# First layer of a two-layer decoder trunk: latent rows turned by VectorE's blocks and HBM, latent products seven units later, the attentions' first scores moved

## The chip, the core and the metric

The kernel runs on one core of one Trainium2 chip. Its engines are TensorE (PE, products; PEld is its weight load), VectorE (DVE), ScalarE (ACT), GpSimd (POOL), and SyncE (SP), which only issues DMAs; SPq is its DMA queue. Each engine runs its own list of instructions in order and waits for the others by semaphores. The metric is the device time of the whole program in microseconds (us), median of the runs shown; lower is better.

## The reference

```python
def hybrid_mixer(h, w_in, ...):
    p = h @ w_in
    (cq, ckv, k_rope, mq, mk, mv, rq, rk, rv, rg, g_mla, g_moba, g_ret) = jnp.split(p, IN_SPLIT_IDX, axis=-1)
    o_mla = mla_branch(cq, ckv, k_rope, mla_q_norm, mla_kv_norm, mla_w_q_up, mla_w_kv_up, cos_mla, sin_mla)
    o_moba = moba_branch(mq, mk, mv, cos_moba, sin_moba)
    o_ret = retention_branch(rq, rk, rv, rg, ret_gn_w, ret_gn_b, cos_ret, sin_ret)
    merged = (jax.nn.sigmoid(g_mla) * (o_mla @ w_branch_mla)
              + jax.nn.sigmoid(g_moba) * (o_moba @ w_branch_moba)
              + jax.nn.sigmoid(g_ret) * (o_ret @ w_branch_ret))
    return merged @ w_out
...
def mla_branch(cq, ckv, k_rope, q_norm_g, kv_norm_g, w_q_up, w_kv_up, cos, sin):
    cq = rms_norm(cq, q_norm_g)
    ckv = rms_norm(ckv, kv_norm_g)
    q = (cq @ w_q_up)            # 8 heads of 64 + 32 (rope on the 32)
    kv = (ckv @ w_kv_up)         # 8 heads of 64 (keys) + 64 (values)
    ...                          # rope(k_rope) is shared by the heads
    o = causal_attention(q, k, v, (MLA_NOPE + MLA_ROPE) ** -0.5)
...
for l in range(DEPTH):           # 2 layers; 256 rows of 1024
    h = rms_norm(x, attn_norm[l])
    x = x + hybrid_mixer(h, w_in[l], ...)
    h = rms_norm(x, mlp_norm[l])
    x = x + jnp.square(jax.nn.relu(h @ w_mlp_up[l])) @ w_mlp_down[l]
return rms_norm(x, final_norm)
```

The latent rows are cq (256 columns), ckv (128) and k_rope (32): normalised (the first two) or roped (the third), they are multiplied by the latent weights w_q_up and w_kv_up. With 256 rows, the moba branch is a causal attention of 8 heads of 64 with rope on 16 of the 64. All is float32.

## The kernel before

**Tiling.** The 256 rows are two halves of 128, the width of 1024 is 8 chunks of 128. A weight block is 128 x 1024 numbers, 512 KB. `weight_plan` (line 72 on) lists all blocks in the order of use; SP fetches them into `raw` (7 buffers), ScalarE rounds each to its upper half `whi` (line 287), VectorE subtracts to get the lower half `wlo` (line 289), 6 buffers each. PE makes three products of each pair (upper by upper, upper by lower, lower by upper: `three`, lines 308 to 310). A **unit** is the work on one block: 12 products of 512 columns. A projection of 512 columns is four units (j = 0 to 3) that sum into two accumulator banks, and its `done` step copies them out. There are four banks `acc` and four banks `misc`, each taken in turn, so a bank's next user waits for the copy that empties it.

**The order.** `prog` is the list of units; `at(slot(key, j), step)` hangs a step behind a unit; `run` goes through it once. At the build a scheduler turns this into one list per engine, with its own estimates of durations, except for what is pinned to program order. In layer 0 the units are: `start` 0 to 7 (the latent columns and mq), mk 0 to 3, mv 0 to 3 with the latent units `qrope`, `qnope`, `kvup` among them, gmla0 and gmla1 (the gate of the MLA branch, whose tanh `th` stands in line 695), gmoba0 and gmoba1, rqk, rv, rg, gret0 and gret1, then the branches, `wout` and the MLP.

**Latent rows.** `c_norms` leaves them as rows (`c` and, for the roped k_rope, `krx`). PE needs them turned, as `cTh` and `cTl` (upper and lower half). In layer 0 `c_turn`, at mk 2, turns them by eight PE transposes into two misc banks `pct` (line 956) and splits them from there with the norm's gain (lines 324, 325). In layer 1 VectorE turns them in blocks of 32 x 32 into `cblocks` (line 842), one DMA writes those to HBM (`rowsbounce`, line 844), four read them back so that the whole is turned (`c_fetch`, `read_turned`, line 512, into `cT`), and a plain split follows (line 329); the gain is there multiplied into the latent weights (lines 279 to 283).

**The latent units.** `qrope` makes the rotary part of the queries (`pqr`, copied to `qr`, line 993; `swapped` exchanges quarters by four DMAs into `qkoth`; `qr_rope`, line 1011, writes the roped result into `Q`), `qnope` the rest of `Q`, `kvup` the keys `KK` and values `vml`. `pqr` and `kvup` use misc banks, `qnope` uses acc banks.

**Moba rows.** `moba_rope` ropes mq or mk as rows on VectorE (`rope_rows`, lines 494 to 497), turns them (line 338) and writes them to HBM (line 504); `fetch_turned` reads them back (line 512) as `mqT` and `mkT`; `order_queries` copies mqT into `qkT` on ScalarE (line 520) for the scores.

**Attentions.** `attention` hangs the first four heads' scores at `first`, the other four at `first + gap`, and the turning, writing and reading back of the probabilities at `first + turn` and `first + moved`. The retention branch's turned rows are `rqkT`.

Of the kernel before, what the change touches and what calls it, by code (L numbers as in the profile page):

```python
# [14 lines left out]
P = 128  # L15
D = 1024
S = 256
# [10 lines left out]

TURNED = 2, 3, 0, 1
SEVEN = [(0, 1, 2, 3, 4, 6)] * L  # L30
LATENT = {"qrope": 0, "qnope": 0, "kvup": 2}
EPS = 1e-6
GN_EPS = 1e-5
# [39 lines left out]
def weight_plan():  # L73

    plan = []

    def block(key, name, kt, cols, per):
        for j in range(0, kt, per):
            plan.append(((*key, j // per), name, (j, per), cols))

    def span(c, n):
        return range(c, c + n)

    for l in range(L):
        if l == 0:

            plan.append(((l, "mq", 0), "w_in", (0, 1), C_MQ))
            plan.append(((l, "b0", 0), "w_in", (0, 1), C_MLA))
            for k in range(1, KD):
                plan.append(((l, "b0mq", k), "w_in", (k, 1), [*C_MLA, *C_MQ]))  # L90
        else:
            for j in TURNED:
                plan.append(((l, "b0", j), "w_in", (2 * j, 2), C_MLA))
            block((l, "mq"), "w_in", KD, C_MQ, 2)
        block((l, "mk"), "w_in", KD, C_MK, 2)
        block((l, "mv"), "w_in", KD, C_MV, 2)
        start = len(plan) - 4 + l
        for i, (key, name, kt, cols) in enumerate(
            (("qrope", "mla_w_q_up", 2, C_QROPE), ("qnope", "mla_w_q_up", 2, C_QNOPE), ("kvup", "mla_w_kv_up", 1, C_KV))
        ):  # L100
            block((l, key), name, kt, cols, kt)
            plan.insert(start + 2 * i, plan.pop())
        for i in range(2):
            block((l, "gmla%d" % i), "w_in", KD, span(C_GMLA + 512 * i, 512), 2)
        for i in range(2):
            block((l, "gmoba%d" % i), "w_in", KD, span(C_GMOBA + 512 * i, 512), 2)
        def branch_block(name, i):
            block((l, "b%s%d" % (name, i)), "w_branch_" + name, 4, span(512 * i, 512), 2)

        block((l, "rqk"), "w_in", KD, C_RQK, 2)  # L110
        block((l, "rv"), "w_in", KD, C_RV, 2)
        block((l, "rg"), "w_in", KD, span(C_RG, 512), 2)
        for i in range(2):
            block((l, "gret%d" % i), "w_in", KD, span(C_GRET + 512 * i, 512), 2)
        for name, i in LATE:
            branch_block(name, i)
        for n in range(KD):
            block((l, "wout", n), "w_out", KD, span(P * n, P), KD)
        for kind, i in mlp_order(l):
            if kind == "down" and l < L - 1 and i >= NF - ENDS[l]:  # L120
                half, m = divmod(i - NF + ENDS[l], 2)
                plan.append(((l, "end", half, m), "w_mlp_down", (NF - ENDS[l] + 2 * m, 2), span(512 * half, 512)))
            elif kind == "up":
                g, j = divmod(i, 4)
                plan.append(((l, "up", g, j), "w_mlp_up", (2 * j, 2), span(512 * g, 512)))
            else:
                plan.append(((l, "down", i, 0), "w_mlp_down", (i, 1), range(D)))
    at, offset = {}, 0
    for key, name, (j, n), cols in plan:
        at[key] = (offset, n, len(cols))  # L130
        offset += P * n * len(cols)
    return plan, at, offset
# [15 lines left out]
G_CQ = 0  # L148
# [6 lines left out]
def trunk(ctx: ExitStack, tc: tile.TileContext, gx, wts, consts, gfin, gn, xtok, out):  # L155
# [112 lines left out]
    def fetch(key):  # L268
        if key[1] == "down" and key[2] // 4 in SEVEN[key[0]] and key[2] % 4 > 1:
            return fetch_sums(key)  # L270
        offset, n, c = where[key]
        sz = n * c
        raw = started.pop(key, None)
        if raw is None:
            raw = wp.tile([P, 1024], F32, name="raw", bufs=RAW)
            transfer(key, raw)
        hi = wp.tile([P, 1024], F32R, name="whi", bufs=6)
        lo = wp.tile([P, 1024], F32R, name="wlo", bufs=6)
        if key[0] and key[1] in LATENT:
            parts = [slice(c * j, c * j + c) for j in range(n)]  # L280
            for j, cs in enumerate(parts):
                fetched.append(split(raw[:, cs], hi[:, cs], lo[:, cs], gain(G_CQ + 3 * key[0] + LATENT[key[1]] + j))[0])
            return tuple(part[:, :sz].rearrange("p (k c) -> p k c", k=n) for part in (hi, lo))
        edge = {"b0mq": 416, "mq": 256}.get(key[1], sz) if key[0] == 0 else sz
        parts = (slice(0, edge), slice(edge, sz)) if edge < sz else (slice(0, sz),)
        for cs in parts:
            fetched.append(nc.scalar.activation(hi[:, cs], raw[:, cs], AF.Copy))  # L287
        for cs in parts:
            nc.vector.tensor_sub(lo[:, cs], raw[:, cs], hi[:, cs].bitcast(F32))  # L289
        return (  # L290
            hi[:, :sz].rearrange("p (k c) -> p k c", k=n),
            lo[:, :sz].rearrange("p (k c) -> p k c", k=n),
        )
# [18 lines left out]
    def gain(c):  # L312
        return G[:, c : c + 1]
# [14 lines left out]
    def split_plain(src, hi, lo):  # L328
        return nc.scalar.activation(hi, src, AF.Copy), nc.vector.tensor_sub(lo, src, hi.bitcast(F32))  # L329
# [467 lines left out]
    def layer(l, xn, before):  # L797
# [21 lines left out]
        def c_norms():  # L819
# [4 lines left out]
            for t, (ct, m) in enumerate(c0):  # L824
# [9 lines left out]
                    nc.vector.tensor_copy(dst[:, :, 16 * i : 16 * i + 16], kr[:, 0, :, :])  # L834
                for i, cs in enumerate((slice(0, MLA_QR), slice(MLA_QR, MLA_QR + MLA_KVR))):
                    nc.vector.tensor_scalar(ct[:, cs], ct[:, cs], m[:, 4 + i : 5 + i], s, op0=ALU.mult, op1=ALU.mult)
            if not l:
                return
            blocks = blocks_tile("c")
            for t, (ct, _) in enumerate(c0):  # L840
                for js, row in ((slice(0, 3), ct[:, :384]), (slice(3, 4), krx[t])):
# [99 lines left out]
        def c_turn():  # L941
# [1 line left out]
            mla["Q"] = sb.tile([P, MLA_H, S], F32, name="Q", bufs=1)  # L943
            KK = mla["K"] = sb.tile([P, MLA_H, S], F32, name="KK", bufs=1)
            mla["v"] = [w2k("vml") for _ in range(NT)]
            if l:
                parts = (c[key][:, 0:3, :].rearrange("p j (t a e) -> p (j t) a e", t=NT, a=4) for key in ("h", "l"))
                split_plain(c["T"][:, 0:3].rearrange("p j t a e -> p (j t) a e"), *parts)
                kr = w2k("kr")[:, :S]
                nc.scalar.copy(kr.rearrange("p (t a e) -> p t a e", t=NT, a=4), c["T"][:, 3])  # L950
            else:
                pts = [misc_tile("pct") for _ in range(2)]
                for k in range(4):
                    for t in range(NT):
                        o = pts[k // 2][:, (k % 2) * S + P * t : (k % 2) * S + P * t + P]
                        nc.tensor.transpose(o, c0[t][0][:, P * k : P * k + P] if k < 3 else krx[t], ident)
                for k in range(3):
                    pt = pts[k // 2][:, (k % 2) * S : (k % 2) * S + S]
                    split(pt, c["h"][:, k, :], c["l"][:, k, :], gain(G_CQ + k))
                kr = pts[1][:, S:]  # L960
            for rows, odd in ((slice(0, 64), 1), (slice(64, P), 0)):
                nc.scalar.copy(KK[rows, odd::2, :], kr[rows, None, :].to_broadcast([64, 4, S]))

        if l:
            at(slot("mq", 3), c_fetch)
        at(slot("mk", 0 if l else 2), c_turn)

        def nope(dst, w, ks, copy, bank):
            for b in range(2):
# [45 lines left out]
                nc.vector.tensor_add(mla["Q"][0:64, 2 * b + 1 :: 4, :], qr[rows], qo[rows])  # L1015

        project(l, "mv", xn, 512, moba_done("mv"))
        for i, unit in enumerate((qrope, qnope, kvup)):
            prog.insert(slot("mv", i + l), ((unit.__name__, 0), unit))
        at(slot("mv", l), qr_rope)  # L1020

        omlaT, omobaT, oretT = [], [], []
        th_mla = gates(l, "gmla", xn)
        for i, key in enumerate(("mq", "mk")):
            at(slot("gmla0", 2 + i) if l else slot("mv", i), lambda key=key: moba_rope(key))
            at(slot("gmla1", 1 + i) if l else slot("gmla0", 2 * i), lambda key=key: fetch_turned(key))
        first = slot("gmla0", 0) if l else slot("mv", 3)
        at(first, lambda: omlaT.extend((t4("omlah"), t4("omlal"))))

        def mla_scores(h0):  # L1030
# [4 lines left out]
            return banks  # L1035

        mla_last = attention(
            omlaT, lambda: mla["v"], QKD, first, mla_scores, (), MLA_GAP, MLA_TURN, MLA_MOVED, ("probT", "KK"),
            (l, "rg", 1), range(0, 4) if l else range(4, 8),
        )  # L1040

# [16 lines left out]
            qkT["q", h0] = in_order(qkT["mq"], h0 // 2)  # L1058

        for i in range(2):  # L1060
            at(slot("gmoba0", i) if l else slot("gmla1", 1 + i), lambda i=i: order_queries(4 * i))
        first = slot("gmoba1", 1)
        at(first, lambda: omobaT.extend((t4("omobah"), t4("omobal"))))

        def moba_scores(h0):
# [6 lines left out]
            return banks  # L1072

        moba_last = attention(
            omobaT, lambda: mqkv["mv"], MB_D, first, moba_scores, mla_last, GAP, TURN, MOVED, ("KK", "KK"),
            (l, "bmoba0", 0), () if l else range(0, 4),
        )

# [582 lines left out]
SMALL = 16  # L1661
FIRST = 4
AHEAD = 1
GAP = 8

TURN = [6, GAP + 3]
MOVED = [GAP, GAP + 4]
MLA_GAP = 7
MLA_TURN = [5, MLA_GAP + 4]
MLA_MOVED = [MLA_GAP + 5, MLA_GAP + 8]  # L1670
T4 = 8
RAW = 7
X_TURN = 17, 21
# [82 lines left out]
```

## Time and profile before

| | us |
|---|---|
| time before, median of 3 runs (800.70 to 801.38) | 801.03 |
| the profiled execution | 800.39 |
| its span, first to last instruction | 798.3 |
| PE busy in it | 791.4 |
| DVE busy | 655.3 |
| ACT busy | 492.5 |
| POOL busy | 29.1 |

The granted clock of TensorE is 0.998 of full speed over the span; the DMA queues moved 196.84 MB, 247 GB/s in the mean. A row of the timeline has start, duration, engine, line, operation, output<-input, size and count, and in brackets how long the engine was idle before it and what ended that. A row with a count above 1 covers instructions that follow each other. Matmuls overlap in the pipeline, so from one to the next the starts are to be compared, not the durations. SPq rows are issues of DMAs.

### The profile page before, as it was taken

How to read it: one execution, taken by the hardware profiler on the slowest of the kernel's cores; microseconds unless marked ns; L12 is line 12 of the kernel's file. 1: busy time of each engine (PE TensorE's matmuls, PEld its weight loads, DVE VectorE, ACT ScalarE, POOL GpSimd, SP SyncE). 2: the span in 40 equal slices, each digit the busy share in tenths (PEclk: the TensorE clock that was granted, in tenths of full speed). 3: DMA queues.
4: the chain of work that ended last, by engine and by line, in shares of the span. 5: the costliest groups of instructions: out<-in, count | busy, mean ns of one | idle time of the engine just before them, and what ended most of it. 6: DMA issues, size and time to landing. Idle time of an engine off the chain costs nothing.

```text
span 798.3 us, 11119 instructions
## 1 busy us (share of the span) xinstructions
PE 791.4 (99%) x3802; PEld 657.2 (82%) x3802; DVE 655.3 (82%) x1137; ACT 492.5 (62%) x751; POOL 29.1 (4%) x32
## 2 busy tenths in 40 slices
PE   9999999999999999999999999999999999999996
PEld 7888887888888888888888888888888888888885
DVE  6789679878888888887787599788698879899795
ACT  7786666453557666666485866654545666666562
POOL 0100000000030000000011000000000300000000
PEclk9999999999999999999999999999999999999999
DMA  9979967965677866775858589988665687788751
GB/s 334 371 248 294 303 216 228 307 220 168 226 225 236 270 229 237 261 268 185 307 160 281 182 237 336 312 275 256 226 227 187 195 272 271 239 282 310 248 180 54
DMA packets 72440, 196.84 MB, mean 247 GB/s; under 512 B 8256, under 2 KB 29632, under 8 KB 72384
## 3 DMA queue, kind: packets, MB, share of 16 engines
q1 hardware_dynamic: 71808, 195.27, 74.5%
q10 hardware_dynamic: 576, 0.87, 0.3%
q8 instruction: 30, 0.49, 0.3%
q14 instruction: 26, 0.21, 0.1%
HBM read 172.51 MB, written 23.07 MB: 245 GB/s over the span
## 4 chain that ended last, share of the span: by engine, by line
PE 99%; DMA 0%; ACT 0%; DVE 0%; issue 0%
PE acc L308 19%; PE acc L310 19%; PE acc L309 19%; PE pup L309 8%; PE pup L308 8%; PE pup L310 8%; PE acc L1269 6%; PE acc L879 1%; PE ps_s L1034 1%; PE po L657 1%; PE ps_s L563 1%; PE po L659 0%; PE b L885 0%; DMA raw<-wts 0%; PE ps_r L563 0%; PE b L886 0%
## 5 line engine op out<-in xcount | busy, mean ns | idle before, releaser
L287 ACT ACTIVATE whi<-raw 128x1024 fp32r<-128x1024 f32 (+3 forms) x260 | 261.6, 1020 | 163.5 <-PE acc L310 104.6
L289 DVE TENSOR_TENSOR wlo<-raw,whi 128x1024 fp32r<-128x1024 f32 (+3 forms) x260 | 300.6, 1172 | 61.7 <-ACT whi L287 59.7
L308 PE MATMUL acc<-whi,xs 128*128 128x512 f32 (+1 forms) x384 | 150.1, 392 | 0.0
L309 PE MATMUL acc<-wlo,xs 128*128 128x512 f32 (+1 forms) x384 | 149.1, 389 | 0.0
L310 PE MATMUL acc<-whi,xs 128*128 128x512 f32 (+1 forms) x384 | 148.7, 389 | 0.0
L309 PE MATMUL pup<-wlo,xs 128*128 128x512 f32 x256 | 99.9, 390 | 0.0
L310 PE MATMUL pup<-whi,xs 128*128 128x512 f32 x256 | 99.7, 389 | 0.0
L308 PE MATMUL pup<-whi,xs 128*128 128x512 f32 x256 | 99.4, 389 | 0.0
L308 PEld LDWEIGHTS acc<-whi,xs 128*128 128x128 f32 x384 | 72.1, 188 | 16.1 <-ACT whi L287 0.7
L310 PEld LDWEIGHTS acc<-whi,xs 128*128 128x128 f32 x384 | 72.1, 188 | 14.9 <-DVE xs L325 0.4
L309 PEld LDWEIGHTS acc<-wlo,xs 128*128 128x128 f32 x384 | 72.1, 188 | 14.1
L310 PE MATMUL acc<-whi,sq 128*128 128x512 f32 x184 | 71.9, 391 | 0.0
L308 PE MATMUL acc<-whi,sq 128*128 128x512 f32 x184 | 71.7, 390 | 0.0
L309 PE MATMUL acc<-wlo,sq 128*128 128x512 f32 x184 | 71.6, 389 | 0.0
L310 PEld LDWEIGHTS pup<-whi,xs 128*128 128x128 f32 x256 | 48.1, 188 | 9.9
L309 PEld LDWEIGHTS pup<-wlo,xs 128*128 128x128 f32 x256 | 48.1, 188 | 9.8
L308 PEld LDWEIGHTS pup<-whi,xs 128*128 128x128 f32 x256 | 47.9, 188 | 9.8
L585 ACT ACTIVATE prob<-prob,smx 128x128 f32<-128x128 f32 x64 | 28.3, 444 | 22.4 <-DVE smx L582 22.4
L310 PEld LDWEIGHTS acc<-whi,sq 128*128 128x128 f32 x184 | 34.5, 188 | 7.7 <-DVE sq L329 0.6
L309 PEld LDWEIGHTS acc<-wlo,sq 128*128 128x128 f32 x184 | 34.5, 188 | 7.2
L308 PEld LDWEIGHTS acc<-whi,sq 128*128 128x128 f32 x184 | 34.5, 188 | 7.1
L1269 PE MATMUL acc<-mT,whi 128*128 128x512 f32 (+1 forms) x144 | 35.2, 371 | 0.0
(286 smaller groups left out, 1204.9 us busy)
## 6 DMA issues: line engine op xcount, KB each, us to landing
raw<-wts SPq DMA_DIRECT2D x264, 512.0 KB, 5.0
bounce<-hblocks SPq DMA_DIRECT2D x16, 512.0 KB, 3.7
hturned<-bounce SPq DMA_DIRECT2D x64, 128.0 KB, 3.1
pbounce<-blocks SPq DMA_DIRECT2D x8, 768.0 KB, 5.9
probT<-pbounce SPq DMA_DIRECT2D x32, 192.0 KB, 5.8
raw<-wts SPq DMA_DIRECT2D x5, 464.0 KB, 7.1
raw<-wts SPq DMA_DIRECT2D x4, 416.0 KB, 4.9
dec<-consts SPq DMA_DIRECT2D x2, 768.0 KB, 9.1
```

The source lines that it names most:

```text
L287: fetched.append(nc.scalar.activation(hi[:, cs], raw[:, cs], AF.Copy))
L289: nc.vector.tensor_sub(lo[:, cs], raw[:, cs], hi[:, cs].bitcast(F32))
L308: nc.tensor.matmul(o, ah, bh, start=start, stop=False, **more)
L309: nc.tensor.matmul(o, ah, bl, start=False, stop=False, **more)
L310: nc.tensor.matmul(o, al, bh, start=False, stop=stop, **more)
L563: mm = nc.tensor.matmul(bank[:, o], a[rows, sa], b[rows, sb_], start=True, stop=True)
L585: nc.scalar.activation(p[:, a:b], p[:, a:b], AF.Exp, bias=m[:, 2 + i : 3 + i], scale=d**-0.5, accum_out=m[:, 4 + i : 5 + i])
L657: nc.tensor.matmul(dst, vh, pT[h + j][0], start=True, stop=False)
L879: nc.tensor.matmul(mq[t][:, cs], a[:, P * t : P * t + P], wq[part][:, cs], start=first, stop=stop)
L1034: nc.tensor.matmul(bank[:, o], mla["Q"][:, h, qs], mla["K"][:, h, ks], start=True, stop=True)
L1269: nc.tensor.matmul(o, a, b, start=half == 0 and i == 0, stop=4 * half + n == KD and i == len(jobs) - 1)
```

## The change

In layer 0:

- The latent rows are turned as in layer 1: `c_norms` turns them on VectorE in blocks and writes them to HBM, `c_fetch` (now at mk 2) reads them back, `c_turn` (now at mv 0) splits them plainly. The eight PE transposes go; the gain goes into layer 0's latent weights.
- `SHIFT = 7, 1` sets how many units of mv, gmla0, gmla1 stand ahead of `qrope`; it was 0 in layer 0 and 1 in layer 1. `qrope`, `qnope`, `kvup` now stand ahead of gmla0 3, gmla1 0 and gmla1 1; their weight blocks move alike.
- `moba_rope` of mq and mk moves from mv 0 and 1 to gmla0 2 and 3, `fetch_turned` from gmla0 0 and 2 to gmla1 1 and 2, `order_queries` from gmla1 1 and 2 to gmoba0 0 and 1.
- The MLA attention's first scores move from mv 3 to gmla1 2, and the gap to its second ones falls from 7 units to 4. The moba attention's first scores move from gmoba1 1 to gmoba1 3; its gap falls from 8 to 6, so the second ones stay.

Layer 1 keeps its numbers, now as the second entries of the tables, apart from where in the code its steps are hung (`c_turn` at mk 0 as before).

```diff
+SHIFT = 7, 1
@@ weight_plan
-        start = len(plan) - 4 + l
+        start = len(plan) - 4 + SHIFT[l]
+        for i in range(2):
+            block((l, "gmla%d" % i), "w_in", KD, span(C_GMLA + 512 * i, 512), 2)
...
-        for i in range(2):
-            block((l, "gmla%d" % i), "w_in", KD, span(C_GMLA + 512 * i, 512), 2)
@@ fetch
-        if key[0] and key[1] in LATENT:
+        if key[1] in LATENT:
@@ c_norms
-            if not l:
-                return
             blocks = blocks_tile("c")
@@ c_turn
-            if l:
-                parts = (c[key][:, 0:3, :].rearrange("p j (t a e) -> p (j t) a e", t=NT, a=4) for key in ("h", "l"))
...
-            else:
-                pts = [misc_tile("pct") for _ in range(2)]
-                for k in range(4):
-                    for t in range(NT):
...
-                        nc.tensor.transpose(o, c0[t][0][:, P * k : P * k + P] if k < 3 else krx[t], ident)
-                for k in range(3):
...
-                    split(pt, c["h"][:, k, :], c["l"][:, k, :], gain(G_CQ + k))
-                kr = pts[1][:, S:]
+            parts = (c[key][:, 0:3, :].rearrange("p j (t a e) -> p (j t) a e", t=NT, a=4) for key in ("h", "l"))
+            split_plain(c["T"][:, 0:3].rearrange("p j t a e -> p (j t) a e"), *parts)
+            kr = w2k("kr")[:, :S]
+            nc.scalar.copy(kr.rearrange("p (t a e) -> p t a e", t=NT, a=4), c["T"][:, 3])
...
-        if l:
-            at(slot("mq", 3), c_fetch)
-        at(slot("mk", 0 if l else 2), c_turn)
+        at(slot("mq", 3) if l else slot("mk", 2), c_fetch)
...
-        for i, unit in enumerate((qrope, qnope, kvup)):
-            prog.insert(slot("mv", i + l), ((unit.__name__, 0), unit))
-        at(slot("mv", l), qr_rope)
...
+        units = [(key, j) for key in ("mv", "gmla0", "gmla1") for j in range(4)][SHIFT[l] :]
+        for i, unit in enumerate((qrope, qnope, kvup)):
+            prog.insert(slot(*units[i]), ((unit.__name__, 0), unit))
+        at(slot("mv", 0) if not l else slot("mk", 0), c_turn)
+        at(slot(*units[0]), qr_rope)
         for i, key in enumerate(("mq", "mk")):
-            at(slot("gmla0", 2 + i) if l else slot("mv", i), lambda key=key: moba_rope(key))
-            at(slot("gmla1", 1 + i) if l else slot("gmla0", 2 * i), lambda key=key: fetch_turned(key))
-        first = slot("gmla0", 0) if l else slot("mv", 3)
+            at(slot("gmla0", 2 + i), lambda key=key: moba_rope(key))
+            at(slot("gmla1", 1 + i), lambda key=key: fetch_turned(key))
+        first = slot(*units[3])
...
-            at(slot("gmoba0", i) if l else slot("gmla1", 1 + i), lambda i=i: order_queries(4 * i))
-        first = slot("gmoba1", 1)
+            at(slot("gmoba0", i), lambda i=i: order_queries(4 * i))
+        first = slot("gmoba1", 1 if l else 3)
...
-GAP = 8
-TURN = [6, GAP + 3]
-MOVED = [GAP, GAP + 4]
-MLA_GAP = 7
-MLA_TURN = [5, MLA_GAP + 4]
-MLA_MOVED = [MLA_GAP + 5, MLA_GAP + 8]
+GAP = 6, 8
+TURN = (4, 9), (6, 11)
+MOVED = (7, 10), (8, 12)
+MLA_GAP = 4, 7
+MLA_TURN = (3, 7), (5, 11)
+MLA_MOVED = (6, 10), (12, 15)
```

What the scheduler makes of it is read in the engines' lists (line, operation, output<-input, size, count; the changed kernel's line numbers are one higher or more). First PE at the end of mk and the start of mv, before; `pct` are the transposes.

```order
L310 MATMUL acc<-whi,xs_90 128x512
L956 MATMUL pct<-K,c_330 128x128
L956 MATMUL pct<-K,c_327 128x128
L956 MATMUL pct<-K,c_330 128x128 x2
L956 MATMUL pct<-K,krx_73 128x128
L956 MATMUL pct<-K,krx_74 128x128
L308 MATMUL acc<-whi,xs_90 128x512
```

In the changed list the products on `acc` follow each other there with nothing between. Second, VectorE where the rope of mq stands, before (ahead of it are the splits of the turned latent rows from PSUM):

```order
L325 SCALAR_TENSOR_TENSOR cTl<-pct,GX,cTh 128x256
L289 TENSOR_TENSOR wlo<-raw,whi 128x1024 x2
L494 TENSOR_TENSOR mrot<-mqrows,K 128x256
L494 TENSOR_TENSOR mrot<-mkrows,K 128x256
L495 TENSOR_TENSOR mqrows<-mqrows,K 128x16x16
L495 TENSOR_TENSOR mkrows<-mkrows,K 128x16x16
L497 TENSOR_TENSOR mqrows<-mqrows,mrot 128x16x8 x2
```

and the same place after the change:

```order
L290 TENSOR_TENSOR wlo<-raw,whi 128x1024 x3
L326 SCALAR_TENSOR_TENSOR wlo<-raw,GX,whi 128x256 x2
L290 TENSOR_TENSOR wlo<-raw,whi 128x1024
L330 TENSOR_TENSOR cTl<-cT,cTh 128x768
L495 TENSOR_TENSOR mrot<-mqrows,K 128x256
L496 TENSOR_TENSOR mqrows<-mqrows,K 128x16x16
L498 TENSOR_TENSOR mqrows<-mqrows,mrot 128x16x8 x2
L339 STREAM_TRANSPOSE mqblocks<-mqrows 128x4x4x32 x2
```

The rope of mq stood behind splits of latent rows that come from PE; it now stands directly behind the split of `cT`, which is read back from HBM. Third, ScalarE from the copies of mqT to the tanh of gmla0, before (the rows of `prob`, the first attention's exponentials, lie between):

```order
L854 ACTIVATE mv<-acc,ms 128x512 x2
L287 ACTIVATE whi<-raw 128x1024 x2
L520 COPY qkT<-mqT 128x512 x2
L287 ACTIVATE whi<-raw 128x1024 x2
L585 ACTIVATE prob,smx<-prob,smx 128x128
```

and after:

```order
L325 ACTIVATE whi<-raw,GX 128x1024
L288 ACTIVATE whi<-raw 128x1024
L521 COPY qkT<-mqT 128x512
L288 ACTIVATE whi<-raw 128x1024
L521 COPY qkT<-mqT 128x512
L979 COPY qr<-pqr 128x512
L696 ACTIVATE th<-acc,half 128x512 x2
```

Before, the copies stood at a distance from the tanh, behind the copies of mv; now the tanh of gmla0 follows them directly, with only the copy of `qr` between. Fourth, PE at the start of gmla1 after the change, with the engines that each product waits for:

```order
L309 MATMUL nope<-cTh,whi 128x256 [waits Activation_49]
L310 MATMUL nope<-cTl,whi 128x256
L309 MATMUL acc<-whi,xs_90 128x512 [waits Activation_49]
L310 MATMUL acc<-wlo,xs_90 128x512 [waits DVE_49]
L311 MATMUL acc<-whi,xs_90 128x512
L309 MATMUL acc<-whi,xs_90 128x512
L310 MATMUL acc<-wlo,xs_90 128x512
L309 MATMUL acc<-whi,xs_90 128x512 [waits Activation_49]
```

The first product of gmla1 (the third row) takes the bank that gmla0 filled, and its wait on ScalarE is for the first tanh of gmla0; the eighth row's is for the second. Before, with `qnope` ahead of gmla0, gmla1's banks were those that mv had filled.

More of the change, by code (lines that the diff above doesn't have):

```diff
@@ L945, in c_turn @@
             mla["v"] = [w2k("vml") for _ in range(NT)]
-            if l:
-                parts = (c[key][:, 0:3, :].rearrange("p j (t a e) -> p (j t) a e", t=NT, a=4) for key in ("h", "l"))
-                split_plain(c["T"][:, 0:3].rearrange("p j t a e -> p (j t) a e"), *parts)
-                kr = w2k("kr")[:, :S]
-                nc.scalar.copy(kr.rearrange("p (t a e) -> p t a e", t=NT, a=4), c["T"][:, 3])
-            else:
-                pts = [misc_tile("pct") for _ in range(2)]
-                for k in range(4):
-                    for t in range(NT):
-                        o = pts[k // 2][:, (k % 2) * S + P * t : (k % 2) * S + P * t + P]
-                        nc.tensor.transpose(o, c0[t][0][:, P * k : P * k + P] if k < 3 else krx[t], ident)
-                for k in range(3):
-                    pt = pts[k // 2][:, (k % 2) * S : (k % 2) * S + S]
-                    split(pt, c["h"][:, k, :], c["l"][:, k, :], gain(G_CQ + k))
-                kr = pts[1][:, S:]
+            parts = (c[key][:, 0:3, :].rearrange("p j (t a e) -> p (j t) a e", t=NT, a=4) for key in ("h", "l"))
+            split_plain(c["T"][:, 0:3].rearrange("p j t a e -> p (j t) a e"), *parts)
+            kr = w2k("kr")[:, :S]
+            nc.scalar.copy(kr.rearrange("p (t a e) -> p t a e", t=NT, a=4), c["T"][:, 3])
             for rows, odd in ((slice(0, 64), 1), (slice(64, P), 0)):
                 nc.scalar.copy(KK[rows, odd::2, :], kr[rows, None, :].to_broadcast([64, 4, S]))
-        if l:
-            at(slot("mq", 3), c_fetch)
-        at(slot("mk", 0 if l else 2), c_turn)
+        at(slot("mq", 3) if l else slot("mk", 2), c_fetch)
         def nope(dst, w, ks, copy, bank):
@@ L1037, in layer @@
         mla_last = attention(
-            omlaT, lambda: mla["v"], QKD, first, mla_scores, (), MLA_GAP, MLA_TURN, MLA_MOVED, ("probT", "KK"),
+            omlaT, lambda: mla["v"], QKD, first, mla_scores, (), MLA_GAP[l], MLA_TURN[l], MLA_MOVED[l], ("probT", "KK"),
             (l, "rg", 1), range(0, 4) if l else range(4, 8),
@@ L1074, in layer @@
         moba_last = attention(
-            omobaT, lambda: mqkv["mv"], MB_D, first, moba_scores, mla_last, GAP, TURN, MOVED, ("KK", "KK"),
+            omobaT, lambda: mqkv["mv"], MB_D, first, moba_scores, mla_last, GAP[l], TURN[l], MOVED[l], ("KK", "KK"),
             (l, "bmoba0", 0), () if l else range(0, 4),
```

## The prediction

> **What bounds the kernel now.** I read the profile page first: the engine totals (busy time, share of the span, instructions), then the chain of work that ended last.
>
> ```profile
> PE 791.4 (99%) x3802; PEld 657.2 (82%) x3802; DVE 655.3 (82%) x1137; ACT 492.5 (62%) x751; POOL 29.1 (4%) x32
> PE 99%; DMA 0%; ACT 0%; DVE 0%; issue 0%
> ```
>
> PE is busy for 791.4 of the 798.3 us of the span, and the chain lies on PE for 99%. So time can be won only by taking work from PE or filling its few gaps, and anything that comes late for PE is lost in full: there is no idle time later in which PE could catch up. VectorE, ScalarE and the DMA queue cost nothing until PE has to wait for one of them. The question is therefore what PE waits for after the change. I take the first 70 us of the timeline, engine by engine (columns: start, duration, engine, line and operation, output<-input, count; in brackets the idle time before and what ended it).
>
> **What the change removes from PE.** First the timeline of PE around the eight transposes of the latent rows.
>
> ```profile
> 32.71 0.39 PE L310 MATMUL acc<-whi,xs 128*128 128x512 f32 x1
> ...
> 34.97 0.40 PE L308 MATMUL acc<-whi,xs 128*128 128x512 f32 x1
> 35.21 0.27 PE L956 MATMUL pct<-K,c 128*128 128x128 f32 x1
> ...
> 35.90 0.40 PE L308 MATMUL acc<-whi,xs 128*128 128x512 f32 x1
> ...
> 37.05 0.39 PE L310 MATMUL acc<-whi,xs 128*128 128x512 f32 x1
> 37.46 0.66 PE L956 MATMUL pct<-K,c 128*128 128x128 f32 x4
> ...
> 38.41 0.39 PE L309 MATMUL acc<-wlo,xs 128*128 128x512 f32 x1
> ```
>
> Products of 512 columns start every (34.97 - 32.71)/10 = 0.226 us here. From 34.97 to 35.90 there are three such steps, 0.68, and the rows show 0.93: two transposes cost 0.25. From 37.05 to 38.41 there are two steps, 0.45, and the rows show 1.36: six transposes (the four shown and two of the rotary rows), with PE's wait for the last normalised row among them, cost 0.91. Together **1.2 us go**, all of it on the bound. The same products of the latent rows remain, at the same count, only later, and so do the scores. No other PE work goes.
>
> **What it puts in place.** VectorE turns the rows by blocks, they are written to HBM and read back turned (the c trip). That trip is not new in kind: the moba queries (mq) make one in layer 0 now, and layer 1 makes both. What is new is how they stand in line. In the changed order on VectorE the rope and the turning of mq stand behind the lower half of the turned latent rows (cTl), which waits for the c trip. On ScalarE the tanh of gmla0 (th), which frees the accumulator bank for gmla1's first product, stands behind the two copies of mqT, which wait for the mq trip. So PE's first product of gmla1 waits for **two trips in series**. Before, the mq rope waited for nothing from HBM, and that product waited only for copies of mv.
>
> When is that chain through? The start is on VectorE:
>
> ```profile
> 36.99 0.67 DVE L836 TENSOR_SCALAR c<-c,ssc,ms 128x256 f32<-128x256 f32 x2 [0.59 <-POOL ssc L827]
> 37.58 2.35 DVE L289 TENSOR_TENSOR wlo<-raw,whi 128x1024 fp32r<-128x1024 f32 x2
> 426.88 0.58 DVE L842 STREAM_TRANSPOSE cblocks<-c 128x384 f32<-128x384 f32 x1
> ```
>
> The last norm of the latent rows starts at 36.99 and lets the next instruction start at 37.58; one split follows (2.35/2, 1.17) and two turnings (0.58 each, by layer 1's row): 37.58 + 1.17 + 1.16 = 39.9. The small scaling for which POOL is waited now stands ahead of a split, so the 0.59 in brackets may go: 39.3. I take 39.6.
>
> The trips, from the issue of the write (SPq) to the first reader (ACT), both of layer 1 and that of layer 0:
>
> ```profile
> 52.99 0.33 SPq L504 DMA_DIRECT2D rowsbounce<-mqblocks  x1
> 61.53 0.62 ACT L520 COPY qkT<-mqT 128x512 f32<-128x512 f32 x1 [1.90 <-DMA mqT<-rowsbounce]
> 429.31 0.33 SPq L844 DMA_DIRECT2D rowsbounce<-cblocks  x1
> 439.25 0.85 ACT L329 ACTIVATE cTh<-cT 128x768 fp32r<-128x768 f32 x1 [1.93 <-DMA cT<-rowsbounce]
> 460.71 0.33 SPq L504 DMA_DIRECT2D rowsbounce<-mqblocks  x1
> 472.77 1.14 ACT L520 COPY qkT<-mqT 128x512 f32<-128x512 f32 x2 [2.35 <-DMA mqT<-rowsbounce]
> ```
>
> They are 8.5, 9.9 and 12.1 us long, and in all three the reader waited for the DMA. For c I take its only row, 9.9, and 8.5 as the low end; for mq the row of its own layer, 8.5, and 12.1 as the high end. Between the trips VectorE and ScalarE do this, and behind the second one ScalarE has this ahead of the first tanh:
>
> ```profile
> 440.13 0.96 DVE L329 TENSOR_TENSOR cTl<-cT,cTh 128x768 fp32r<-128x768 f32 x1 [1.55 <-ACT cTh L329]
> 48.38 0.42 DVE L494 TENSOR_TENSOR mrot<-mqrows,K 128x256 f32<-128x256 f32 x1
> 49.06 0.41 DVE L495 TENSOR_TENSOR mqrows<-mqrows,K 128x256 f32<-128x256 f32 x1
> 49.73 0.48 DVE L497 TENSOR_TENSOR mqrows<-mqrows,mrot 128x128 f32<-128x128 f32 x2
> 51.67 1.30 DVE L338 STREAM_TRANSPOSE mqblocks<-mqrows 128x512 f32<-128x512 f32 x2
> 473.81 2.95 ACT L287 ACTIVATE whi<-raw 128x1024 fp32r<-128x1024 f32 x3
> 445.41 0.56 ACT L993 COPY qr<-pqr 128x512 f32<-128x512 f32 x1
> 467.35 0.67 ACT L695 ACTIVATE th<-acc,half 128x512 f32<-128x512 f32 x1
> ```
>
> Between the trips: 440.13 - 439.25 = 0.88, then 0.96 + 0.42 + 0.41 + 0.48 + 1.30, in all 4.45; consecutive rows overlap by some hundredths, so 4.4. Behind the second: two copies 1.14 (472.77), one rounding 2.95/3 = 0.98, the copy of the rotary queries 0.56, the tanh 0.67, in all 3.35, so 3.3. The chain ends at 39.6 + 9.9 + 4.4 + 8.5 + 3.3 = **65.7**.
>
> When is PE there? Its latent products have their pace in the timeline of PE:
>
> ```profile
> 45.11 0.28 PE L309 MATMUL pqr<-cTl,whi 128*128 128x256 f32 x1
> ...
> 48.83 0.28 PE L310 MATMUL nope<-cTh,wlo 128*128 128x256 f32 x1
> ```
>
> There are 31 steps in 3.72 us, 0.12 each. Without the transposes, from the product at 34.97: 3 x 0.227 = 0.68 to the end of mk; seven units (four of mv, three of gmla0) of 12 products, 2.72 each, 19.04; qrope, 12 x 0.12 = 1.44; the last unit of gmla0, 2.72; and 26 products of qnope and kvup that the order has ahead of gmla1, 3.12. That is 34.97 + 0.68 + 19.04 + 1.44 + 2.72 + 3.12 = **62.0**. PE would wait 65.7 - 62.0 = **3.7 us**. The ends: 39.3 + 8.5 + 4.4 + 8.5 + 3.3 = 64.0, a wait of 2.0; and 39.9 + 9.9 + 4.4 + 12.1 + 3.3 = 69.6, a wait of 7.6. Product qrope itself needs cTl: 39.6 + 9.9 + 0.88 + 0.96 = 51.3, against PE at 34.97 + 0.68 + 19.04 = 54.7, so the first trip by itself is covered by 3.4 us.
>
> **The rest of the change, at nothing.** VectorE's four turnings (two of 0.58, two smaller) and ScalarE's copies take the place of three splits with gain from PSUM; both engines have idle time and PE does not wait there. The gain on layer 0's latent weights splits their two halves apart, as layer 1 does. One write and four reads more on the DMA queue are 1 MB of 196.84, and up to seven raw buffers of weights lie between the queue and ScalarE. The moba attention's first scores are now two units later and its first values stay where they were, so the retention scores come up behind a shorter run of ScalarE work:
>
> ```profile
> 135.34 0.62 ACT L520 COPY qkT<-rqkT 128x512 f32<-128x512 f32 x1 [0.32 <-DMA rqkT<-rowsbounce]
> 139.89 0.49 PE L563 MATMUL ps_r<-rqkT,qkT 64*128 64x256 f32 x2
> ```
>
> The turned retention rows are copied by 135.96 and used at 139.89, a cover of 3.9 us; work that slips by less costs nothing, and what slips further is paid one for one. I take nothing. Layer 1's order stays.
>
> **The sum.** The profiled execution took 800.39; minus 1.2 plus 3.7 is 802.9. The median of the three runs, 801.03, is 0.64 above the profiled one, so I forecast 803.5.
>
> **The rivals.**
> 1. The trips are short, no wait is left, and only the transposes go: 801.03 - 1.2 = 799.8. This needs the two trips in 62.0 - 39.6 - 4.4 - 3.3 = 14.7 us, 7.35 each. For it speaks the page's table of DMA issues (KB each, median us to landing), with rows of another trip of the same size:
>
> ```profile
> bounce<-hblocks SPq DMA_DIRECT2D x16, 512.0 KB, 3.7
> hturned<-bounce SPq DMA_DIRECT2D x64, 128.0 KB, 3.1
> ```
>
> With the four issues of the reads between them (52.99's trip has 8.5 where these give 6.8) they could come near it; against it speak the three trips above, none under 8.5. The Trainium skill's "DMA: Bandwidth & Descriptors", section "Anatomy of one DMA — SWDGE (gpsimd) path", gives about 2.0 us a DMA plus the bytes at 436 GB/s. That is, as an estimate from that page, 3.2 us for the write and as much for four reads together, 6.4 a trip, and it would make this rival the likeliest; the rows of this kernel, whose transfers go by another path and beside weight blocks, are 8.5 to 12.1, and the measurement decides.
>
> 2. The wait is there, and PE runs slowly for a while behind it. The only row of a slow clock is the start:
>
> ```profile
> 0.77 3.43 PE L777 MATMUL warm<-const-bfloat16-1.0 128*128 128x512 bf16 x8 [0.77 <-PEq L1749]
> ```
>
> Eight products of 512 columns take 3.43 us after idleness, 0.43 each against 0.227 later. If a wait of 3.7 us brought that state back for as long, 3.43 x (1 - 0.227/0.43) = 1.6 us would be added: 805.1. The Trainium skill's "TensorE: Matmul & The Clock Gate", section "Part 1: The HAM clock gate (the "warmup" mystery)", has the clock halved after an idle window of about 3.4 us in windows that run freely. By it a wait this near to one window seldom fills one; no row here shows an idle PE after the start, so the chance stays small.
>
> 3. A second wait, at the first scores behind gmla1. The queries' rotary halves are swapped by DMA, and the copy ahead of that swap stands behind the late copies of mqT. In layer 1:
>
> ```profile
> 446.47 0.52 SPq L529 DMA_DIRECT2D qkoth<-qr  x1
> 453.31 0.69 DVE L1011 TENSOR_TENSOR qr<-qr,K 128x512 f32<-128x512 f32 x1 [3.58 <-DMA qkoth<-qr]
> ```
>
> The swap takes 6.8 us until its reader starts. Counted from mqT's landing M, the copy ahead of it is done at M + 1.14 + 0.98 + 0.56 = M + 2.7 and the swap at M + 9.5; two multiplications (0.69 each), a split (1.17) and a first add of about 0.5 on VectorE make the first queries whole near M + 12.6. PE, released at M + 3.3, has 36 products of 512 columns and six more of kvup (42 x 0.227 = 9.5) and ten latent ones (1.2) up to the scores, which it reaches at M + 14.0. That is a margin of 1.4 us. The mq trips differ by 3.6 between the layers; a swap slower by 3 us would add 1.6: 805.1.
>
> 4. The change doesn't do what it says. The orders of the two programs show the transposes gone and the steps moved, so I give it nothing.
>
> **How the numbers follow.** The wait of 2.0 to 7.6 us by itself (801.8 to 807.4, 803.5 likeliest) has 0.64; no wait or less than 2.0 (799.8 to 801.8) 0.18; the slow clock 0.06; the second wait 0.09; faster still, where removed work in the first 40 us brings more than the transposes, 0.03. The first two cases hold 0.82, so the range is 799.8 to 807.4. A measurement of this kernel tells about 0.2%, 1.6 us, from no change: 799.4 to 802.6. Slower is then most of the first case (waits over 2.8 us, 0.47 of 0.64) and cases two and three of the rivals: 0.62. Same is the rest of the first, and no wait: 0.35. Faster 0.03.
>
> **What would show it.** Right: in the profile after, no L956 rows; an idle gap of PE of 2 to 7 us near 62 that ends with ScalarE's th; ahead of it on ScalarE a wait for mqT of several us, on VectorE a wait for cTh near 49; from there on every unit late by the wait less 1.2. Wrong: PE gapless from 35 to 70 (rival 1); products at 0.43 behind the gap (rival 2); a gap at the first L1034 scores (rival 3). The forecast fails if either trip is well under 8 us, or if the mq copies don't hold up the tanh.

## The result and the profile after

The changed kernel takes 808.92 us (median of 5 runs, 807.97 to 810.74) against 800.70 before (median of 5, 800.23 to 801.38): a ratio of 1.0107, 95% interval 1.009 to 1.0124. It is slower, as forecast, but by 8.2 us where 2.5 were forecast, and outside the range. The profiled execution took 808.61 us. Its page begins:

```profile
PE 794.0 (98%) x3794; PEld 659.1 (82%) x3794; DVE 657.0 (81%) x1141; ACT 493.7 (61%) x752; POOL 28.7 (4%) x32
```

PE has eight instructions fewer, yet is busy 2.6 us longer (791.4 before), in a span that grew by 8.2 (806.5). So there are two losses: 5.6 us more in which PE does nothing, and products that take longer. The timeline of PE shows both at one place, and the windows (length; busy time and number of instructions of PE, PEld, DVE, ACT and POOL in turn; granted clock; busy share of the DMA engines; GB/s) say at what clock PE ran.

```profile
62.11 0.28 PE L310 MATMUL nope<-cTl,whi 128*128 128x256 f32 x1
67.38 0.80 PE L309 MATMUL acc<-whi,xs 128*128 128x512 f32 x1 [4.99 <-ACT th L696]
67.97 0.63 PE L310 MATMUL acc<-wlo,xs 128*128 128x512 f32 x1
68.40 0.63 PE L311 MATMUL acc<-whi,xs 128*128 128x512 f32 x1
68.83 0.63 PE L309 MATMUL acc<-whi,xs 128*128 128x512 f32 x1
```

```profile
62.20:67.40 5.20, 0.21 (x3) 0.02 (x1) 1.59 (x3) 3.23 (x6) 0.00 (x0) 0.92 0.95 312
67.40:73.40 6.00, 6.00 (x16) 4.84 (x17) 5.89 (x10) 5.20 (x8) 0.00 (x0) 0.50 0.58 158
73.40:80.00 6.60, 6.60 (x34) 5.60 (x34) 5.36 (x7) 5.99 (x9) 0.00 (x0) 1.00 1.07 306
```

PE is done with the 26th latent product at 62.2 and starts gmla1 at 67.4, released by the tanh of gmla0: a gap of some 5.2 us (4.99 in the row, which counts from the modelled end of the product before). Behind it products of 512 columns start 0.43 apart, not 0.227, and the granted clock is 0.50 for 6.0 us, then 1.00 again. Twelve such products and three latent ones cost 12 x 0.20 + 3 x 0.09 = 2.7 us.

The chain ahead of that tanh, on VectorE, the DMA queue and ScalarE:

```profile
38.48 0.33 SPq L843 DMA_DIRECT2D rowsbounce<-cblocks  x1
39.59 1.46 SPq L216 DMA_DIRECT2D raw<-wts  x2
44.45 1.75 SPq L513 DMA_DIRECT2D cT<-rowsbounce  x4
50.66 0.85 ACT L330 ACTIVATE cTh<-cT 128x768 fp32r<-128x768 f32 x1 [5.33 <-DMA cT<-rowsbounce]
55.18 0.33 SPq L505 DMA_DIRECT2D rowsbounce<-mqblocks  x1
64.17 0.62 ACT L521 COPY qkT<-mqT 128x512 f32<-128x512 f32 x1 [4.92 <-DMA mqT<-rowsbounce]
66.64 0.69 ACT L696 ACTIVATE th<-acc,half 128x512 f32<-128x512 f32 x1
```

The c trip takes 50.66 - 38.48 = 12.2 us, what lies between the trips 4.5, the mq trip 9.0, and the tanh is done 3.2 us later. The same products stand against each other in the two traces by 7.1 us behind 110 us, by 7.7 behind 262 us, by 8.6 behind 467: two small waits further back, of which a second profile speaks below.

### The profile page after: what moved, and what is told of

Its sections match the earlier page's. It is cut to its first block, busy times and chain, and to the rows that moved or that the text cites. A ratio compares the mean times of both kernels' runs of the same rounds, so it can differ in the third digit from the quotient of the medians.

```text
span 806.5 us, 11109 instructions
## 1 busy us (share of the span) xinstructions
PE 794.0 (98%) x3794; PEld 659.1 (82%) x3794; DVE 657.0 (81%) x1141; ACT 493.7 (61%) x752; POOL 28.7 (4%) x32
## 4 chain that ended last, share of the span: by engine, by line
PE 88%; DMA 5%; DVE 3%; ACT 2%; issue 1%; SPq 1%; POOL 0%; ACTq 0%; DVEq 0%
PE acc L309 16%; PE acc L311 16%; PE acc L310 16%; PE pup L309 8%; PE pup L310 8%; PE pup L311 8%; PE acc L1256 6%; PE acc L878 1%; DMA rowsbounce<-cblocks 1%; PE ps_s L1021 1%; DMA cT<-rowsbounce 1%; DVE wlo L290 1%; PE po L658 1%; PE ps_s L564 1%; DMA qkoth<-qr 1%
## 5 line engine op out<-in xcount | busy, mean ns | idle before, releaser
L288 ACT ACTIVATE whi<-raw 128x1024 fp32r<-128x1024 f32 (+4 forms) x257 | 259.3, 1021 | 161.3 <-PE acc L311 102.2
L290 DVE TENSOR_TENSOR wlo<-raw,whi 128x1024 fp32r<-128x1024 f32 (+4 forms) x257 | 297.7, 1174 | 58.9 <-ACT whi L288 56.3
```

## Experiments

Theory A: the gap comes from two trips in series ahead of gmla0's tanh, and the slow products come from the gap. Theory B: the tanh is late because ScalarE and VectorE are held by the c trip, whatever mqT does. Each short diff is against the changed kernel if nothing else is said; "run 2" is the kernel of experiment 2. Ratios are to the kernel before.

**1. The mq rope early.**

```diff
-            at(slot("gmla0", 2 + i), lambda key=key: moba_rope(key))
-            at(slot("gmla1", 1 + i), lambda key=key: fetch_turned(key))
+            at(slot("gmla0", 2 + i) if l else slot(("mk", "mv")[i], 3 * (1 - i)), lambda key=key: moba_rope(key))
+            at(slot("gmla1", 1 + i) if l else slot("gmla0", 2 * i), lambda key=key: fetch_turned(key))
```

> The changed kernel with one edit: in layer 0 the mq rope, its turning and its write stand at mk 3 (mk's at mv 0) and the reads back at gmla0 0 and 2, so that the mq trip no longer stands behind the c trip. Theory A (PE's 5.0 us wait comes from two trips in series, c then mq, ahead of gmla0's tanh; the slow products behind it come from the idle time): ScalarE's copy of mqT waits for no DMA, PE's gap near 62 us is under 0.5 us, no product of 512 columns starts 0.43 after the one before, time 799.5 to 802.5. Theory B (the tanh is late because ScalarE and VectorE are held by the c trip and the latent splits behind it, whatever mqT does): the gap stays at 3 us or more and the time at 806 or more.

804.4 us, ratio 1.0044 (1.0027 to 1.0060): better by 4.5 than the change, but not what A alone gives. mqT is there when ScalarE wants it. What remains, by the list of PE's waits (total, times, longest) and the window behind the gap:

```profile
PE acc L309 <- ACT th L696: 1.4, 1, 1.4
PE warm L778 <- PEq L1736: 0.8, 1, 0.8
PE acc L311 <- DVE sq L330: 0.5, 1, 0.5
PE pqr L310 <- DVE cTl L330: 0.5, 1, 0.5
PE ps_s L1021 <- DVE Q L1000: 0.5, 2, 0.3
```

```profile
64.40:70.00 5.60, 5.60 (x30) 4.87 (x31) 1.82 (x2) 5.50 (x8) 0.00 (x0) 1.00 1.08 212
```

The gap is 1.4 us and the clock behind it is 1.00. On ScalarE cT came at 53.94 (its write went out 2.8 us later, at 41.25, behind mq's turnings), and 9.7 us of work stood between that and the tanh at 63.67 without a pause. So B holds for a smaller part: ScalarE's list piles up behind its wait for cT (in run 7, where the copies of mqT no longer stand in that pile, 0.3 us of the 1.4 are left). A is the larger one.

**2. The tanh first.** Both trips stay in series, but ScalarE copies mqT behind the tanh.

```diff
+                if half == 0 and key == "gmla":
+                    behind["queries"] = [tanh]
...
-            qkT["q", h0] = in_order(qkT["mq"], h0 // 2)
+            with ExitStack() as pinned:
+                for ins in () if l else behind["queries"]:
+                    pinned.enter_context(tc.issue_after(ins.ins))
+                qkT["q", h0] = in_order(qkT["mq"], h0 // 2)
```

> The changed kernel with one edit: in layer 0 ScalarE's copies of mqT are issued behind the first tanhs of gmla0; both trips stay in series. Theory A: mqT still lands near 64 us and ScalarE still waits for it, but the tanhs are done before PE reaches gmla1, so the gap goes (under 0.5 us) and with it the slow products; 799.5 to 802.5. Theory B: the tanhs stay late, 806 or more. Theory C (the late mqT also holds up the queries' copies and so the scores): the gap moves to the first scores, 2 us or more, 803 to 806.

802.0 us, ratio 1.0013 (1.0003 to 1.0022), 6.9 below the change. The gap at gmla1 and the half clock are gone, with mqT still copied at 65.15. What Theory C names is there, 1.9 us large (PE's waits; then the timeline of the queue and of VectorE):

```profile
PE ps_s L1023 <- DVE Q L1002: 1.9, 1, 1.9
```

```profile
62.60 2.50 SPq L530 DMA_DIRECT2D qkoth<-qr  x4
71.68 0.69 DVE L999 TENSOR_TENSOR qr<-qr,K 128x512 f32<-128x512 f32 x1 [5.42 <-DMA qkoth<-qr]
```

The swap of the rotary queries takes 9.1 us here, from 62.60 to 71.68, and PE, now on time, waits 1.9 us for the queries. The profiled execution, 803.87, is the slowest of the ten; it has three more waits, of 0.5 to 0.8 us, behind 450 us.

**3. PE turns the rows again, all moves kept.** The transposes in `c_turn` and the gain at the split, as before; `SHIFT`, slots and tables as in the change.

```diff
+                        nc.tensor.transpose(o, c0[t][0][:, P * k : P * k + P] if k < 3 else krx[t], ident)
...
+                    split(pt, c["h"][:, k, :], c["l"][:, k, :], gain(G_CQ + k))
...
-        at(slot("mv", 0) if not l else slot("mk", 0), c_turn)
+        at(slot("mk", 0 if l else 2), c_turn)
```

> The changed kernel with the latent rows of layer 0 turned by PE transposes again (gain at the split, as before), everything else where the change put it. Theory A: no c trip, so the mq rope waits for nothing from HBM and the gap near 62 us goes; the transposes come back with their 1.2 us: 800.5 to 803. If the gap has another cause in the moved steps (order of the scores, the tables), it stays, 806 or more.

801.11 us, ratio 1.0005 (0.9995 to 1.0014). Without the c trip the longest wait that is left at gmla1 is 0.3 us. The moves of units, scores and tables by themselves cost nothing and win nothing that the interval could show; in the profile of this run PE waits 0.7 us in all, in three places, besides the start.

**4. The gap filled.** 22 products of constants on a misc bank, ahead of gmla1.

```diff
+        def fill():
+            pf = misc_tile("fill")
+            for i in range(22):
+                mm = nc.tensor.matmul(
+                    pf, nc.const_aps.tensor(1.0, [P, P], BF16), nc.const_aps.tensor(1.0, [P, 512], BF16), start=True, stop=True
+                )
+                tc.keep_in_program_order(mm)
...
+            prog.insert(slot("gmla1", 0), (("fill", 0), fill))
```

> The changed kernel with 22 products of constants (128x512 in bf16, result unused) ahead of gmla1's first product, where PE idles. Theory A (the slow products are the clock's answer to the idle time): the 22 products take some 4.8 us, the rest of the wait for the tanh stays under 1 us, the products behind it start every 0.227 us, and the time falls by 2.7 us against the change alone, to 805.5 to 806.8. Rival (the slow products come from their operands or from DMA traffic at that time): they stay at 0.43, 808 to 810.

805.46 us, ratio 1.0055 (1.0040 to 1.0070), 3.5 below the change, just under what was expected. In the profiles, PE is 4.7 us behind the kernel before at 110 us, in place of 7.1: 2.4 us are won here; the rest lies further back, where the change's profile has its two small waits and this one has none. The same two windows as in the changed kernel:

```profile
62.20:67.40 5.20, 4.87 (x23) 1.99 (x20) 1.51 (x2) 3.13 (x6) 0.00 (x0) 1.00 0.93 316
67.40:73.40 6.00, 5.92 (x31) 5.11 (x32) 5.86 (x11) 5.88 (x9) 0.00 (x0) 1.00 0.55 156
```

The tanh comes as late as ever, the DMA share behind it is the same (0.55 to 0.58), but with PE busy in the gap the clock stays at 1.00 and 31 instructions fit where 16 did. The slow products come from PE's idleness, and the clock's part of the loss goes without the wait being any shorter.

**5. The turning alone, on the kernel before.** Rows turned by VectorE and HBM, `c_fetch` at mk 2, `c_turn` at mk 3; units, scores and tables of before.

```diff
-        if key[0] and key[1] in LATENT:
+        if key[1] in LATENT:
...
-            if not l:
-                return
...
-        if l:
-            at(slot("mq", 3), c_fetch)
-        at(slot("mk", 0 if l else 2), c_turn)
+        at(slot("mq", 3) if l else slot("mk", 2), c_fetch)
+        at(slot("mk", 0 if l else 3), c_turn)
```

> The kernel before with one part of the change alone: layer 0's latent rows turned by VectorE and HBM (read back at mk 2, split at mk 3), the latent units, the attentions and the tables where they were. With a c trip of 12.2 us from about 38.5, cTl is whole near 52.5. The order has 148 products of 512 columns ahead of the first latent product (126 before), so PE is there near 46.3. Theory A (the trip has to be covered by units between): PE waits some 6 us for cTl, and products behind it are slow for 3 to 5 us (2 to 3 us more): 806 to 812. Rival (a trip without weights in its way is as short as 8.5, the rows of before): 2.5 us of wait and no slow products, 802 to 803.

805.57 us, ratio 1.0058 (1.0044 to 1.0072), just under the range of Theory A. The c trip is 12.4 us (38.25 to 50.63), PE waits 5.1 for cTh, and the clock is halved behind it, for 3.4 us, mostly on short products (PE's waits; the window behind the gap):

```profile
PE pqr L308 <- ACT cTh L329: 5.1, 1, 5.1
```

```profile
51.50:54.80 3.30, 3.28 (x13) 3.08 (x14) 0.96 (x1) 3.23 (x4) 0.00 (x0) 0.50 0.18 68
```

In the change PE has no wait at the latent products, so the moves do cover the c trip there; the change moved the wait from there to the tanh, with a second trip behind the first.

**6. The tanh first, and the first scores a unit later.** Against run 2:

```diff
-        first = slot(*units[3])
+        first = slot(*units[3 if l else 4])
...
-MLA_GAP = 4, 7
-MLA_TURN = (3, 7), (5, 11)
-MLA_MOVED = (6, 10), (12, 15)
+MLA_GAP = 3, 7
+MLA_TURN = (3, 6), (5, 11)
+MLA_MOVED = (6, 9), (12, 15)
```

> The run with the tanh first, with one more edit: the MLA attention's first scores in layer 0 one unit later (gmla1 3, gap 3, so that the second stay at gmoba0 2; its tables moved to suit). There PE waited 1.9 us for the last swap of the rotary queries at the first scores, and 0.3 at the next. Theory: one unit is 2.7 us of cover, the wait at the first scores goes, nothing else moves, and what is left is the transposes' gain: 2 us below the run with the tanh first, 799.5 to 800.5 (before 801.0). Rival (the second scores or the probabilities' trip then come late): 801.5 to 803.

799.86 us, ratio 0.9988 (0.9979 to 0.9996). PE waits for nothing but the start:

```profile
PE warm L780 <- PEq L1741: 0.8, 1, 0.8
```

It starts the same products 0.61 us later than before at the start of the execution and 0.55 us earlier behind 110 us: 1.16 us won, the transposes. This version is faster than both kernels, than the one before by 0.9 us, which the interval only just tells from nothing.

**7. The same with the mq rope early as well.** Against run 6, the edit of run 1.

> The same with the mq rope early as well (mk 3), so that both of the edits that each took the long gap away stand together, with the later scores. If the rest of the gap in the run with the early rope (1.4 us at gmla0's tanh) came from ScalarE's work piled up behind its wait for cT, with the copies of mqT among it, it shrinks to under 0.5 us; but the c write goes out 2.8 us later there, which leaves the wait of 0.5 us for cTl: 800 to 801.5, not better than the scores later alone.

800.96 us, ratio 1.0008 (0.9999 to 1.0017). PE waits 0.6 for cTl and 0.3 for the tanh, as the later write of c lets expect. With the tanh first, the early rope has nothing left to give and costs a late c.

**8. The rotary queries copied by VectorE.** Against run 2:

```diff
-            nc.scalar.copy(mla["qr"], acc)
+            (nc.scalar.copy if l else nc.vector.tensor_copy)(mla["qr"], acc)
```

> The run with the tanh first, with the rotary queries (qr) of layer 0 copied from PSUM by VectorE in place of ScalarE. If the wait of 1.9 us at the first scores comes from the copy's place in ScalarE's list, behind four roundings, the swap is issued earlier only as far as VectorE is free: its list has the copy behind its splits, so at most 1 us is won: 801 to 802. If the swap's own 9.1 us on the queue is what counts, nothing changes: 801.5 to 802.5.

801.39 us, ratio 1.0006 (0.9997 to 1.0015); the wait at the first scores is 1.6 in place of 1.9, and the swap takes 9.1 us again (62.27 to 71.36). The two forecasts overlap, and the time lies in what the first one allows and just under the second, so the run doesn't decide between them. Little is won by the copy's engine; cover by a unit (run 6) is what takes the wait away.

**9. Fewer weights ahead of the c trip.**

```diff
-RAW = 7
+RAW = 5
```

> The changed kernel with RAW = 5 in place of 7: two weight blocks fewer stand on the DMA queue ahead of the c write, one fewer between the write and the reads. Theory D (the c trip took 12.2 us in place of 9.9 because weights running ahead fill the DMA engines there: share 0.96 to 1.01 against 0.81 in layer 1's trip): the share falls and the c trip takes 9 to 10.5 us, so the chain to gmla0's tanh ends 2 to 3 us earlier, PE's gap is 2 to 3.5 us, and fewer or no products are slow: 802.5 to 806, if no weights come late elsewhere. Rival (the trip is long by its own packets, whatever runs beside it): it stays near 12, the gap at 5, the time at 807.5 to 810.

814.16 us, ratio 1.0171 (1.0154 to 1.0188): the time is far outside, the trip inside Theory D. The windows over the c trip of the changed kernel (two rows), of layer 1's trip in the kernel before, and of this run:

```profile
38.50:44.50 6.00, 6.00 (x28) 4.97 (x27) 4.21 (x5) 2.21 (x4) 0.00 (x0) 1.00 0.96 283
44.50:50.60 6.10, 6.10 (x28) 5.07 (x27) 1.23 (x1) 0.82 (x1) 0.00 (x0) 1.00 1.01 274
```

```profile
429.30:439.20 9.90, 9.90 (x45) 8.22 (x44) 4.86 (x4) 4.53 (x5) 0.00 (x0) 1.00 0.81 254
```

```profile
38.80:49.30 10.50, 10.50 (x48) 8.68 (x48) 3.36 (x3) 1.10 (x2) 0.00 (x0) 1.00 0.86 284
```

The share of the DMA engines (the last number but one) falls from about 1 to 0.86, and the c trip to 49.26 - 38.81 = 10.4 us, near layer 1's 9.9 at 0.81. But the order changed as well: the turning of mq fell behind splits that wait for ScalarE, its write went out at 59.32, ten us behind cT, and the gap became 7.1 us. So the c trip grew shorter with fewer weights beside it, and the time of this run says nothing of it. The other traces agree as far as the latent rows go: with seven buffers, layer 0's c trip took 11.6 to 12.9 us in nine profiles, at shares of 0.95 to 1.02, and layer 1's took 9.2 to 10.8 in thirteen, at 0.75 to 0.87. The mq trip of layer 0 doesn't follow the share: in the kernel before it took 8.5 us at 0.92 and, in the second profile, 10.1 at 0.78. The share alone is no rule for a trip's length, and what else sets it stays open.

**10. Both kernels once more.**

> The changed kernel once more, for a second profile. If the small steps in which its first profile lost 0.6 us at 262 (the layer's MLP, waiting for a split of its squares) and 0.8 at 464 (layer 1's first scores, waiting for the queries) belong to the order that the change leaves, they are here again within 0.2; if they come from how transfers happen to fall in one execution, they are of other sizes or at other places. The gap at gmla1 and the half clock behind it are expected again (4 to 6 us; 2 to 3 us).

> The kernel before once more. Its first profile had no such steps. If they come from how transfers fall, this one may show some of up to 1 us in layer 1 or in the MLP; if they belong to the change, it has none again.

The change: 808.29 us in this execution, with one wait that counts, and the clock at half in the window behind it.

```profile
PE acc L309 <- ACT th L696: 6.2, 1, 6.2
```

```profile
68.70:74.00 5.30, 5.26 (x12) 4.13 (x13) 5.19 (x9) 4.77 (x7) 0.00 (x0) 0.50 0.60 114
```

The trips are 12.7 (38.66 to 51.36) and 9.6 (55.89 to 65.53). Neither the 0.6 us at 262 nor the 0.8 at 464 of the first profile are there, so they belong to single executions. The kernel before, 800.17 us, has no such wait this time either; why some executions have them and others don't stays open.

## Why the prediction was wrong

- **What bounds the kernel** was right: PE, gapless, with nothing given back later. The loss made near 62 us stands in full to the end.
- **The transposes' 1.2 us** was right: 1.16 in run 6.
- **Where PE waits and for whom** was right: gmla1's first product, for the tanh of gmla0, behind two trips in series. Run 2, which only puts the tanh ahead of the second trip's reader, takes the gap away; run 3, which takes the first trip away, does too. PE's own arrival, forecast at 62.0, was 62.2.
- **The size of the wait** was too small, 3.7 for 5.2 and 6.3 us. The term that failed is the trips': for c "I take its only row, 9.9", and the 8.5 for mq, measured 12.2 and 9.0, in the second profile 12.7 and 9.6. The turned blocks were ready 1.1 us earlier than taken (38.5 for 39.6); 4.4 between and 3.3 behind were right to some 0.1. The row of 9.9 came from a stretch in which the DMA engines were 81% busy; over the c trip of layer 0, where weights run ahead into seven buffers, they were full (0.96 and 1.01). Half of this could have been read beforehand: in the trace of before, the window from 38.5 to 44.5 us has a share of 0.89, and the trip itself adds 1 MB there; but the next one, to 50.6, has 0.56, and didn't give it away. The high end of the range of waits, 7.6, did hold.
- **The clock** is the step that carried the time out of the range: the sum has nothing for it, and it was given to a rival with 0.06. It was sized at 1.6 us and measured 2.7 and 2.6 in the two profiles of the change. The passage that failed reads "a wait this near to one window seldom fills one": that was weighed for the likeliest wait of 3.7 alone, while the forecast's own waits ran to 7.6, and a wait of 5 to 6 us is not near one window of 3.4. With the true waits, -1.2 + 5.2 + 2.7 = 6.7 and -1.2 + 6.3 + 2.6 = 7.7, the two profiled executions, 8.2 and 8.1 us longer in span than the kernel before profiled beside them, are explained up to 1.5 us of small waits in the first and 0.4 in the second.
- **The range** ended at 807.4, the largest wait without a slow clock. The two go together: a wait long enough to stand at its upper end is also one that halves the clock, so the range should have carried the sum. Run 4, in which the tanh comes as late and the clock doesn't fall, took 805.46, inside the range.
- **The rivals.** No wait: did not happen; the estimate from the Trainium skill's "DMA: Bandwidth & Descriptors", section "Anatomy of one DMA — SWDGE (gpsimd) path", of 6.4 us a trip is well short of what the trips of the change take beside weights (9.0 to 12.7), and the measurement decides. The second wait at the scores: not in the change, since PE was late itself and the swap took 4.0 us there (issued at 66.76, read at 70.78; the scores began at 81.03 without a wait), but it was the next thing behind: 1.9 us in run 2. The forecast's margin of 1.4 us doesn't apply there, since it counts from mqT's landing and the swap of run 2 goes out ahead of that; what cost the 1.9 us is a swap of 9.1 in place of 6.8 before a PE that had lost no time.
- **The rest at nothing** was right: run 3 has all moves, and its ratio to before is 1.0005, with 1 inside the interval.

## What to carry to other kernels

The length of a trip through memory read in one place doesn't carry over to another: the c trip's 9.9 us became 12.2 where the DMA engines were full. Give such a term the spread of all rows of its kind, ask what load it will meet, and count how many trips stand in series ahead of an instruction that frees a bank. An engine that works in order passes one wait on to everything behind it, so look first at what stands between a late reader and the next thing the bound engine needs; putting the tanh ahead of a copy that nobody needed yet won 6.9 us, the clock's part included. Where PE is the bound, an idle stretch of 5 us or more cost more than itself here, some 1.7 us more in run 5 (half of the 3.4 at half clock) and 2.7 in the change, because the clock fell and took time to return. So when a forecast's waits may reach 5 us, price the clock in the same range.

## What the runs showed of the hardware

The half clock comes in a quantum. By the clock records in the traces, PE's clock was at 0.5 for 6.83 us in the first profile of the change (66.60 to 73.43), for 6.83 in the second (67.24 to 74.07) and for 6.83 in run 9 (67.57 to 74.40, gap 7.1), but for 3.41 in run 5 (51.38 to 54.79, gap 5.1). That is once or twice 3.4 us, and it agrees with the Trainium skill's "TensorE: Matmul & The Clock Gate", section "Part 1: The HAM clock gate (the "warmup" mystery)", which has free-running windows of 3.4 us. In steps of 3.4 us, the change looks like this:

```profile
63.20:66.60 3.40, 0.00 (x0) 0.00 (x0) 0.82 (x1) 2.43 (x4) 0.00 (x0) 1.00 0.99 371
66.60:70.00 3.40, 2.62 (x6) 2.14 (x7) 3.30 (x8) 3.37 (x7) 0.00 (x0) 0.50 0.36 105
70.00:73.40 3.40, 3.40 (x11) 2.72 (x11) 3.36 (x5) 2.64 (x4) 0.00 (x0) 0.50 0.76 213
```

The clock falls at the end of a step in which PE did nothing (0.00), stays at half through one in which PE was busy for 2.6 us, and is back behind one in which it was busy throughout. All four falls stand at the end of 3.41 us without any PE work, and all four returns behind a step in which PE was busy for 3.27 us or more. This explains why the gap of 5.1 us in run 5 cost one step and the 5.2 of the change two: in run 5 PE began again 0.14 us into the step behind the fall and kept it busy for 3.27 us, in the change 0.78 into it, which left 2.6. So what a gap costs depends on where it falls in the steps. Gaps of 1.4 us (run 1) and 1.9 (run 2) cost no clock; no run here shows where between 1.9 and 5.1 us it begins to cost.
